# The gated unit of a state space branch: output blocks in the outer loop, chunks of positions inside

## The chip, the cores and the metric

The kernel runs on one core of a Trainium2 chip. The metric is device time in microseconds (us). The engines are TensorE (PE, with its weight loads as PEld), VectorE (DVE), ScalarE (ACT), GpSimd (POOL) and SyncE (SP). Each engine takes its instructions in the order in which they were written into its own queue; SP's queue issues most of the DMAs, ACT's and POOL's queues issue some.

## The reference, cut to what matters

One inference step of a one-layer decoder trunk, for a prompt of 1024 positions and 8 sample positions, 1032 in all. One branch of the layer is a diagonal state space scan followed by a gated unit; only the unit's last lines are touched here:

```
y = y.reshape(nb, seq_len, SSM_WIDTH) + d_skip.astype(f32) * uf
y = jax.nn.gelu(y)
y = y * jax.nn.sigmoid(y @ w_glu.astype(f32) + b_glu.astype(f32))
```

SSM_WIDTH is 512, so `w_glu` is 512 x 512. The branch's output is later multiplied by `w_ssm_proj`, gated and merged with an attention branch.

## The kernel before, in words

Positions are handled in three chunks of 344 (`NCH` = 3, `CH` = 344). A product in full precision is made of three products of rounded parts: every float32 operand is split into a high part (a cast on ACT, line 143 for weights) and a low part (a subtraction on DVE, line 144), and `mm3` issues high x high, high x low and low x high for each slice of 128 inputs (line 158). A block of weights comes through `loadw`: a DMA from SP (line 139) into one of two raw buffers, `r0` and `r1` in turn, then the cast and the subtraction into one of four pairs of buffers (`w2`/`w3`, `w4`/`w5`, `w6`/`w7`, `w8`/`w9`, in turn). A raw buffer is free for the next load when its subtraction is done; a pair is free when the matmuls of the block that used it are done. While pieces of a large cache copy are left, `loadw` also puts one of them into ACT's queue (line 868) with each load.

The program runs in stages: a first feed-forward part, the state space scan in eight batches (which writes `y` to `y_d` in DRAM), then `head(0, 0)` (query, key and value tiles of the first attention head pair), then `glu`, then six attention units, each with the `head` of the next one between its steps, then `ssm_proj` and the rest. `glu` loops over the three chunks. For each it loads the chunk of `y` (`yc`, 128 x 4 x 344, 688 KB), splits it into `yh` and `yl` in four pieces each (lines 547 and 548), and then, for each of four output blocks, loads the 512 x 128 block of `w_glu` (256 KB), multiplies (12 matmuls into one of three `pm` banks), takes tanh on ACT (line 553), multiplies by `y` on DVE (line 554) and stores the 128 x 344 result to `yg_d` from SP (line 555). The result tile `sg` has two buffers. So each block of `w_glu` is loaded and split three times, twelve loads in all. `ssm_proj` reads `yg_d` back much later (line 1165, tiles `P`).

The order of the instructions on each engine is not only that of the code: a scheduler merges `glu` with the tail of `head(0, 0)`, with the first steps of the first attention unit (`unit`, lines 645 to 690) and with the weight loads of `head(0, 1)` (`in_w_in`, 512 KB each), and fixes the order when the program is built.

Of the kernel before, what the change touches and what calls it, by code (L numbers as in the profile page):

```python
# [8 lines left out]
F32 = mybir.dt.float32  # L9
F32R = mybir.dt.float32r  # L10
I32 = mybir.dt.int32
AF = mybir.ActivationFunctionType
ALU = mybir.AluOpType
# [5 lines left out]
CH = 344  # L19
NCH = 3  # L20
# [39 lines left out]
class Step:  # L60
# [88 lines left out]

    def mm3(s, p, W, A, kts, first=True, last=True):  # L150

        nc = s.nc
        h, l = W
        n = 3 * len(kts)
        i = 0
        for kw, ka in kts:
            for w, a in ((h, A[0]), (h, A[1]), (l, A[0])):
                nc.tensor.matmul(p, w[:, kw], a[:, ka], start=first and i == 0, stop=last and i == n - 1)  # L158
                i += 1

    def dense(s, W, c, kts=None, A=None):
        p = s.pm.tile([128, 512], F32, name="pm")
        s.mm3(p[:, :CH], W, A or (s.ah[c], s.al[c]), kts or [(k, k) for k in range(KT)])
        return p[:, :CH]
# [6 lines left out]
    def ffn(s, hp, tmp, wg, wu, wd, xT, after, fill=None, lg=4):  # L171
# [17 lines left out]
        def down(fs):  # L189
            W = [s.loadw(wd[0][128 * f:128 * f + 128, :].rearrange("p (m q) -> p m q", q=128)) for f in fs]  # L190
            last = fs[-1] == NF - 1
            if last:
                order = [(m, c) for c in range(NCH) for m in range(KT)]
            else:
                order = [(m, c) for m in range(KT) for c in range(NCH)]
            for m, c in order:
                p = s.pm.tile([128, 512], F32, name="pm")[:, :CH]
                for i, f in enumerate(fs):
                    s.mm3(p, W[i], H[f], [(m, c)], i == 0, i == len(fs) - 1)
                nc.vector.scalar_tensor_tensor(xT[c][:, m], p, 0.5, xT[c][:, m], op0=ALU.mult, op1=ALU.add)  # L200
                if last:
                    after(c, m)
# [335 lines left out]
    def glu(s, gp):  # L538

        nc = s.nc  # L540
        for ch in range(NCH):
            cs = slice(CH * ch, CH * ch + CH)
            y = gp.tile([128, 4, CH], F32, name="yc", bufs=2)
            nc.sync.dma_start(y, s.y_d.rearrange("(m p) n -> p m n", p=128)[:, :, cs])
            yh, yl = gp.tile([128, 4, CH], F32R, name="yh", bufs=2), gp.tile([128, 4, CH], F32R, name="yl", bufs=2)
            for m in range(4):
                nc.scalar.copy(yh[:, m], y[:, m])
                nc.vector.tensor_sub(yl[:, m], y[:, m], yh[:, m])
            for m in range(4):
                W = s.colw(s.i['w_glu'], 128 * m, 4)  # L550
                p = s.dense(W, ch, [(k, k) for k in range(4)], (yh, yl))
                t = gp.tile([128, CH], F32, name="sg", bufs=2)
                nc.scalar.activation(t, p, AF.Tanh, bias=s.bglu[:, m:m + 1], scale=0.5)
                nc.vector.scalar_tensor_tensor(t, t, 1.0, y[:, m], op0=ALU.add, op1=ALU.mult)
                nc.sync.dma_start(s.yg_d[128 * m:128 * m + 128, cs], t)

    def ssm_finish(s, sp):
        nc = s.nc
# [1146 lines left out]
```

## Time and profile before

| | |
|---|---|
| median of three runs | 2382.05 us (2378.92 to 2386.34) |
| profiled execution, its own time | 2376.9 us |
| its span | 2375.0 us |
| PE busy / PEld busy | 97% / 93% of the span |
| DVE / ACT / POOL busy | 57% / 33% / 14% |
| mean granted clock of TensorE | 0.986 of full speed |

The table is read as follows. PE is the engine that is nearly always busy, and the other engines matter where PE waits for them. The share of 97% is an average over stages. A matmul's end is modelled in the records, and neighbours overlap, so a stretch with PE "busy" throughout can still hold more or fewer matmuls; counting them is the surer way. The profiled execution is 5.15 us below the median of the three runs.

### The profile page before, as it was taken

What the parts mean: (1) busy time and instruction counts of PE and PEld (TensorE: products, weight loads), DVE (VectorE), ACT (ScalarE), POOL (GpSimd) and SP (SyncE); (2) the same over time, 40 slices, a digit from 0 to 9 for tenths busy, and PEclk for the clock granted to TensorE, in tenths of its full rate; (3) what the DMA queues carried; (4) which work ended last, traced back from release to release, by engine and by line L of the source; (5) the groups of instructions that cost most, each with busy time, mean ns of one, the idle gap of its engine ahead of it and who ended that gap; (6) DMA issues with size and microseconds to landing.
All of it is one profiled execution on the core that took longest, in us unless ns stands there. A gap on an engine that the chain in (4) does not pass through costs nothing.

```text
span 2375.0 us, 37141 instructions
## 1 busy us (share of the span) xinstructions
PE 2296.6 (97%) x14409; PEld 2203.8 (93%) x14409; DVE 1359.9 (57%) x2929; ACT 787.7 (33%) x1506; POOL 337.0 (14%) x929
## 2 busy tenths in 40 slices
PE   7999999999999889989999998999999999999999
PEld 6999999999999889978888887899899999999999
DVE  7655544354433734455566536488866666664564
ACT  6211112111112434455443533235433333333222
POOL 3056777000000300000000000210000000000100
PEclk8999999999999999999999999999999999999999
DMA  5333334242323367561142126667334334367553
GB/s 141 101 102 115 110 113 132 85 122 82 112 77 121 129 171 223 176 214 33 57 119 76 40 87 174 219 233 233 116 125 129 119 119 149 119 256 265 193 174 126
DMA packets 300198, 325.73 MB, mean 137 GB/s; under 512 B 38822, under 2 KB 265494, under 8 KB 297462
## 3 DMA queue, kind: packets, MB, share of 16 engines
q1 hardware_dynamic: 277478, 189.94, 26.8%
q0 software_dynamic: 18864, 85.21, 10.1%
q10 hardware_dynamic: 3680, 48.22, 6.6%
q8 instruction: 113, 1.85, 0.3%
q14 instruction: 63, 0.52, 0.1%
HBM read 243.52 MB, written 123.78 MB: 155 GB/s over the span
## 4 chain that ended last, share of the span: by engine, by line
PE 65%; issue 21%; DMA 5%; DVE 5%; POOL 2%; ACT 1%; SPq 0%; ACTq 0%; POOLq 0%; DVEq 0%
PE pm L158 49%; PE pm L1560 9%; PE ps L671 2%; POOL hs_d L1376 2%; DMA r<-in_w_o_dram 1%; PE acc L687 1%; PE pT L680 1%; DMA r<-in_w_in_dram 1%; PE pn L972 1%; DVE xn L128 1%; DMA P<-yg_d 1%; DVE w L144 1%; DMA r<-in_w_ssm_proj_dram 1%; DMA w<-w_d 0%; DMA xr<-in_x_prompt_dram 0%
## 5 line engine op out<-in xcount | busy, mean ns | idle before, releaser
L158 PE MATMUL pm<-ah,w 128*128 128x344 f32 x4192 | 1006.8, 324 | 19.4 <-ACT ut L1141 11.0
L158 PEld LDWEIGHTS pm<-ah,w 128*128 128x128 f32 x4192 | 725.4, 189 | 37.6 <-ACT ut L1141 11.3
L158 PE MATMUL pm<-al,w 128*128 128x344 f32 x2384 | 719.3, 324 | 5.8 <-ACT al L1173 3.1
L158 PEld LDWEIGHTS pm<-al,w 128*128 128x128 f32 x2384 | 441.9, 190 | 13.1 <-issue 6.8
L158 PE MATMUL pm<-hh,w 128*128 128x344 f32 x1056 | 253.7, 321 | 0.0
L143 ACT CAST w<-r 128x1024 fp32r<-128x1024 f32 (+1 forms) x124 | 120.5, 978 | 373.8 <-PE pm L158 350.9
L144 DVE TENSOR_TENSOR w<-r,w 128x1024 fp32r<-128x1024 f32 (+1 forms) x124 | 142.6, 1152 | 159.3 <-ACT w L143 153.8
L1242 ACT CAST w<-r 128x1024 fp32r<-128x1024 f32 (+1 forms) x130 | 125.7, 968 | 286.8 <-PE pm L1348 171.4
L158 PEld LDWEIGHTS pm<-hh,w 128*128 128x128 f32 x1056 | 183.6, 188 | 0.4
L1348 PE MATMUL pm<-ah,w 128*128 128x344 f32 x1056 | 181.8, 320 | 1.2 <-ACT ah L1242 0.7
L1348 PE MATMUL pm<-e,w 128*128 128x344 f32 x1056 | 178.7, 320 | 1.0 <-DVE w L1243 1.0
L200 DVE SCALAR_TENSOR_TENSOR xT<-pm,xT 128x344 f32<-128x344 f32 x240 | 122.0, 515 | 93.4 <-PE pm L158 93.2
L1243 DVE TENSOR_TENSOR w<-r,w 128x1024 fp32r<-128x1024 f32 (+1 forms) x130 | 145.6, 1121 | 48.9 <-ACT w L1242 48.6
L1348 PEld LDWEIGHTS pm<-ah,w 128*128 128x128 f32 x1056 | 169.3, 188 | 1.8 <-ACT ah L1242 1.0
L1348 PEld LDWEIGHTS pm<-e,w 128*128 128x128 f32 x1056 | 168.6, 188 | 1.5 <-DVE w L1243 1.3
L158 PE MATMUL pm<-hl,w 128*128 128x344 f32 x528 | 169.5, 321 | 0.0
L184 DVE TENSOR_TENSOR h<-h,pm 128x344 f32<-128x344 f32 x66 | 33.8, 512 | 189.1 <-PE pm L158 189.1
L1348 PE MATMUL pm<-al,w 128*128 128x344 f32 x792 | 137.6, 322 | 2.6 <-ACT p L1428 2.6
L1348 PEld LDWEIGHTS pm<-al,w 128*128 128x128 f32 x792 | 128.0, 189 | 3.4 <-ACT p L1428 2.9
L158 PEld LDWEIGHTS pm<-hl,w 128*128 128x128 f32 x528 | 99.1, 188 | 0.2
L1376 POOL DMA_DIRECT2D hs_d<-hs x55 | 37.6, 683 | 426.4 <-DVE hs L1243 412.4
L1180 POOL DMA_DIRECT2D rs<-g_d x24 | 12.9, 541 | 532.6 <-DVE rs L103 389.5
(426 smaller groups left out, 3022.9 us busy)
## 6 DMA issues: line engine op xcount, KB each, us to landing
out_dram<-in_cache_kv_w_dram ACTq DMA_DIRECT2D x64, 512.0 KB
hs_d<-hs POOLq DMA_DIRECT2D x44, 688.0 KB, 4.5
r<-in_w_gate_dram SPq DMA_DIRECT2D x44, 512.0 KB
r<-in_w_up_dram SPq DMA_DIRECT2D x44, 512.0 KB
r<-in_w_in_dram SPq DMA_DIRECT2D x38, 512.0 KB
r<-in_w_down_dram SPq DMA_DIRECT2D x36, 512.0 KB
r<-in_w_o_dram SPq DMA_DIRECT2D x24, 512.0 KB
al<-hs_d POOLq DMA_DIRECT2D x7, 1376.0 KB, 6.7
```

What stands on the lines that cost most here:

```text
L128: nc.vector.scalar_tensor_tensor(xn, xT[c][:, k], s.gains[:, z, k:k + 1], r, op0=ALU.mult, op1=ALU.mult)
L143: nc.scalar.copy(h[:, :k], raw[:, :k])
L144: nc.vector.tensor_sub(l[:, :k], raw[:, :k], h[:, :k])
L158: nc.tensor.matmul(p, w[:, kw], a[:, ka], start=first and i == 0, stop=last and i == n - 1)
L184: nc.vector.tensor_mul(h, h, pu)
L200: nc.vector.scalar_tensor_tensor(xT[c][:, m], p, 0.5, xT[c][:, m], op0=ALU.mult, op1=ALU.add)
L671: nc.tensor.matmul(p[h][:, :nk], qT[hs, s.block(g, b)], kT[hs, ks], start=True, stop=True)
L1242: s.nc.scalar.copy(hi, x)
L1243: s.nc.vector.tensor_sub(lo, x, hi)
L1348: nc.tensor.matmul(p, W[w][:, k], B[:, a, k], start=first and k == 0 and z == 0, stop=k == n - 1 and z == 2, skip_group_check=True)
L1376: nc.gpsimd.dma_start(s.hs_d[i:i + n, j].rearrange("i p z n -> p i (z n)"), t[:, :n].rearrange("p i z n -> p i (z n)").bitcast(F32))
L1560: nc.tensor.matmul(p[m], W[wz][:, m], t[:, jj, az], start=e == 0 and k == 0, stop=e == n - 1 and k == 2, skip_group_check=True)
```

## The change

The loop over the four output blocks goes outside and the loop over the three chunks inside. All three chunks of `y` are loaded and split first, each with one cast and one subtraction over 128 x 1376 (through `parts`, lines 1242 and 1243 of the kernel before), and stay on chip, and each block of `w_glu` is loaded once and used for all three chunks. The result tile `sg` has four buffers and not two.

```diff
     def glu(s, gp):
 
         nc = s.nc
+        Y, P = [], []
         for ch in range(NCH):
-            cs = slice(CH * ch, CH * ch + CH)
-            y = gp.tile([128, 4, CH], F32, name="yc", bufs=2)
-            nc.sync.dma_start(y, s.y_d.rearrange("(m p) n -> p m n", p=128)[:, :, cs])
-            yh, yl = gp.tile([128, 4, CH], F32R, name="yh", bufs=2), gp.tile([128, 4, CH], F32R, name="yl", bufs=2)
-            for m in range(4):
-                nc.scalar.copy(yh[:, m], y[:, m])
-                nc.vector.tensor_sub(yl[:, m], y[:, m], yh[:, m])
-            for m in range(4):
-                W = s.colw(s.i['w_glu'], 128 * m, 4)
-                p = s.dense(W, ch, [(k, k) for k in range(4)], (yh, yl))
-                t = gp.tile([128, CH], F32, name="sg", bufs=2)
+            y = gp.tile([128, 4, CH], F32, name=f"yc{ch}")
+            nc.sync.dma_start(y, s.y_d.rearrange("(m p) n -> p m n", p=128)[:, :, CH * ch:CH * ch + CH])
+            yh, yl = (gp.tile([128, 4, CH], F32R, name=f"{x}{ch}") for x in ("yh", "yl"))
+            s.parts(y, yh, yl)
+            Y.append(y)
+            P.append((yh, yl))
+        for m in range(4):
+            W = s.colw(s.i['w_glu'], 128 * m, 4)
+            for ch in range(NCH):
+                p = s.dense(W, ch, [(k, k) for k in range(4)], P[ch])
+                t = gp.tile([128, CH], F32, name="sg", bufs=4)
                 nc.scalar.activation(t, p, AF.Tanh, bias=s.bglu[:, m:m + 1], scale=0.5)
-                nc.vector.scalar_tensor_tensor(t, t, 1.0, y[:, m], op0=ALU.add, op1=ALU.mult)
-                nc.sync.dma_start(s.yg_d[128 * m:128 * m + 128, cs], t)
+                nc.vector.scalar_tensor_tensor(t, t, 1.0, Y[ch][:, m], op0=ALU.add, op1=ALU.mult)
+                nc.sync.dma_start(s.yg_d[128 * m:128 * m + 128, CH * ch:CH * ch + CH], t)
```

The changed file has one line more, so lines behind the loop carry a number higher by one. What the scheduler makes of it is seen at three places.

The first place is SP's queue from the load of the fourth weight block on. `yc` are loads of `y`, `r0` and `r1` the raw buffers of weights, `yg_d` the stores of the unit. Before:

```order
L139 DMA r1_10767<-in_w_glu_dram 128x4x128
L544 DMA yc_10683<-y_d_59 128x4x344
L544 DMA yc_10791<-y_d_59 128x4x344
L139 DMA r0_10803<-in_w_glu_dram 128x4x128
L139 DMA r1_10827<-in_w_glu_dram 128x4x128
L139 DMA r0_10851<-in_w_glu_dram 128x4x128
L555 DMA yg_d_60<-sg_10715 128x344
L139 DMA r1_10875<-in_w_glu_dram 128x4x128
L555 DMA yg_d_60<-sg_10739 128x344
L139 DMA r0_10911<-in_w_glu_dram 128x4x128
L555 DMA yg_d_60<-sg_10763 128x344
L139 DMA r1_10935<-in_w_glu_dram 128x4x128
```

And of the change:

```order
L139 DMA r1_10875<-in_w_glu_dram 128x4x128
L544 DMA yc0_10683<-y_d_59 128x4x344
L544 DMA yc1_10689<-y_d_59 128x4x344
L544 DMA yc2_10695<-y_d_59 128x4x344
L139 DMA r0_11158<-in_w_in_dram 128x8x128
L139 DMA r1_11298<-in_w_in_dram 128x8x128
L556 DMA yg_d_60<-sg_10721 128x344
L556 DMA yg_d_60<-sg_10738 128x344
L139 DMA r0_11438<-in_w_in_dram 128x8x128
L556 DMA yg_d_60<-sg_10755 128x344
```

The third chunk of `y` moves up behind the second, eight loads of `w_glu` are gone, and the weights of `head(0, 1)` (`in_w_in`) take their places in the queue.

The second place is ACT's queue at the first results of the unit: `sg` is the tanh that empties a `pm` bank, CAST the high part of a weight block. Before:

```order
L143 CAST w2_10806<-r0_10803 128x512
L553 ACTIVATE sg_10715<-pm_10702,bglu_103 128x344
L868 DMA out_8_dram<-in_cache_kv_w512_dram 16x8160
L970 ACTIVATE rs0_10507<-kT_10436 128x344
L143 CAST w4_10830<-r1_10827 128x512
L553 ACTIVATE sg_10739<-pm_10726,bglu_103 128x344
L868 DMA out_8_dram<-in_cache_kv_w512_dram 16x8192
L143 CAST w6_10854<-r0_10851 128x512
L99 ACTIVATE rs0_10511<-pT_10509,eps_90 128x344
L100 ACTIVATE rs1_10512<-rs0_10511,seed_92 128x344
L553 ACTIVATE sg_10763<-pm_10750,bglu_103 128x344
```

And of the change:

```order
L554 ACTIVATE sg_10721<-pm_10708,bglu_103 128x344
L971 ACTIVATE rs0_10507<-kT_10436 128x344
L554 ACTIVATE sg_10738<-pm_10725,bglu_103 128x344
L143 CAST w2_11161<-r0_11158 128x1024
L554 ACTIVATE sg_10755<-pm_10742,bglu_103 128x344
L869 DMA out_8_dram<-in_cache_kv_w512_dram 16x8160
L99 ACTIVATE rs0_10511<-pT_10509,eps_90 128x344
L100 ACTIVATE rs1_10512<-rs0_10511,seed_92 128x344
L554 ACTIVATE sg_10779<-pm_10766,bglu_103 128x344
L101 ACTIVATE rs2_10513<-rs1_10512 128x344
L554 ACTIVATE sg_10796<-pm_10783,bglu_103 128x344
```

Before, a cast of a `w_glu` block stands ahead of every tanh. After, one cast of a twice as large `w_in` block stands ahead of every third tanh, the one of the last chunk.

The third place is SP's queue in `ssm_proj`, some 450 us later, where `P` are the loads of `yg_d`, `w_d` and `w` belong to the attention's `combine`, and `g_d` are stores of gates. Before:

```order
L1165 DMA P_15292<-yg_d_60 128x4x86
L959 DMA g_d_61<-gt_15096 128x344
L1165 DMA P_15302<-yg_d_60 128x4x86
L1165 DMA P_15304<-yg_d_60 128x4x86
L736 DMA w_d_63<-cw_15024 16x384
L959 DMA g_d_61<-gt_15124 128x344
L1165 DMA P_15314<-yg_d_60 128x4x86
L750 DMA w_15037<-w_d_63 64x4x128 x2
```

And of the change:

```order
L1166 DMA P_15226<-yg_d_60 128x4x86
L1166 DMA P_15236<-yg_d_60 128x4x86
L960 DMA g_d_61<-gt_15030 128x344
L1166 DMA P_15238<-yg_d_60 128x4x86
L737 DMA w_d_63<-cw_14958 16x384
L1166 DMA P_15248<-yg_d_60 128x4x86
L960 DMA g_d_61<-gt_15058 128x344
L751 DMA w_14971<-w_d_63 64x4x128 x2
```

Two loads of `P` move ahead of a store of gates. Elsewhere behind the unit, too, instructions of the same kinds change places by a few positions; none is added or removed there but the pieces of the cache copy, which follow the loads.

## Rows read from the trace of the kernel before

**Rows 1.** The page: span, and busy time of PE

```profile
span 2375.0 us, 37141 instructions
PE 2296.6 (97%) x14409; PEld 2203.8 (93%) x14409; DVE 1359.9 (57%) x2929; ACT 787.7 (33%) x1506; POOL 337.0 (14%) x929
```

**Rows 2.** Busy time of each engine by stretch of 40 us

```profile
core 0: us, PE busy (x) PEld busy (x) DVE busy (x) ACT busy (x) POOL busy (x), PEclk, DMA share, GB/s
...
980.00:1020.00 40.00, 40.00 (x254) 39.18 (x253) 22.61 (x49) 21.68 (x46) 0.19 (x1) 1.00 0.47 139
1020.00:1060.00 40.00, 29.67 (x170) 25.81 (x169) 24.22 (x53) 18.73 (x35) 0.00 (x0) 1.00 0.84 260
1060.00:1100.00 40.00, 40.00 (x259) 32.79 (x258) 24.45 (x75) 23.97 (x66) 0.00 (x0) 1.00 0.16 47
```

**Rows 3.** What PE waited for, 1015 to 1061 us

```profile
PE pm L158 <- ACT sg L553: 5.1, 5, 2.0
PE pT L647 <- DVE sk L645: 3.2, 1, 3.2
```

**Rows 4.** Timeline of ACT: start us, length us, instruction, idle before it

```profile
1002.69 0.48 ACT L547 CAST yh<-yc 128x344 fp32r<-128x344 f32 x1 [2.14 <-DMA yc<-y_d]
...
1004.61 1.61 ACT L547 CAST yh<-yc 128x344 fp32r<-128x344 f32 x4
...
1025.67 0.62 ACT L143 CAST w<-r 128x512 fp32r<-128x512 f32 x1 [5.15 <-PE pm L158]
...
1027.26 0.53 ACT L553 ACTIVATE sg<-pm,bglu 128x344 f32<-128x344 f32 x1
...
1046.05 1.04 ACT L143 CAST w<-r 128x1024 fp32r<-128x1024 f32 x1 [2.15 <-DMA r<-in_w_in_dram]
```

**Rows 5.** Timeline of SP's queue: issues of DMAs

```profile
998.41 1.00 SPq L544 DMA_DIRECT2D yc<-y_d  x2
...
1020.91 0.37 SPq L139 DMA_DIRECT2D r<-in_w_glu_dram  x1
...
1029.43 1.24 SPq L139 DMA_DIRECT2D r<-in_w_glu_dram  x1
...
1041.19 0.38 SPq L139 DMA_DIRECT2D r<-in_w_in_dram  x1
```

**Rows 6.** Timeline of PE

```profile
1015.38 0.58 PE L158 MATMUL pm<-yh,w 128*128 128x344 f32 x1
...
1027.84 0.42 PE L158 MATMUL pm<-yh,w 128*128 128x344 f32 x1 [2.03 <-ACT sg L553]
...
1033.99 1.04 PE L612 MATMUL pT<-ident,vT 128*128 128x128 f32 x8
...
1050.29 0.43 PE L158 MATMUL pm<-ah,w 128*128 128x344 f32 x1 [0.53 <-ACT sg L553]
...
1059.49 0.28 PE L647 MATMUL pT<-ident,sk 128*24 128x128 f32 x1 [3.19 <-DVE sk L645]
1059.70 0.90 PE L671 MATMUL ps<-kT,qT 64*128 64x256 f32 x4
1060.53 0.43 PE L158 MATMUL pm<-ah,w 128*128 128x344 f32 x1
```

**Rows 7.** The chain that ended last, 960 to 1110 us: start us, us, what

```profile
1015.81 6.44 PE pm L158 x41
1022.25 0.58 PE pT L972 x2
```

**Rows 8.** What PE waited for, 1061 to 1460 us

```profile
PE acc L687 <- ACT P L682: 1.3, 1, 1.3
```

**Rows 9.** Instructions of line 1242: count, ns min/median/max, first and last start

```profile
L1242 ACT CAST al<-xT x3: 1332/1347/1350, 1622.6 to 1649.2; 128x1376 fp32r<-128x1376 f32 x3
```

**Rows 10.** Busy time by stretch, as rows 2, in `ssm_proj`

```profile
1460.00:1500.00 40.00, 31.43 (x181) 25.34 (x180) 25.30 (x58) 14.03 (x34) 2.15 (x4) 0.85 0.51 122
```

**Rows 11.** The chain that ended last, 1440 to 1520 us

```profile
1491.84 4.51 DMA P<-yg_d
```

## The prediction

> **What bounds the kernel now.** I read the page first: PE is busy for 2296.6 of 2375.0 us [rows 1], so a change pays only where PE stands still. The table of stretches says where that is around the gated unit: in 1020 to 1060 us PE is busy for 29.67 of 40 us, with full stretches on either side and the granted clock at 1.00 in all three [rows 2]. So 10.33 us are idle by the record, and no clock is lost there.
>
> What PE waits for there is the tanh on ACT that empties its banks, 5.1 us in five waits, and at the end the small copies `sk` on DVE, 3.2 us in one [rows 3]. Both are late because of weights. On ACT's timeline a cast of a `w_glu` block starts at 1025.67 after 5.15 us of idling; the view names PE as the releaser, but the cast's data came from a load that SP had issued only about 6 us before, so I put this wait down to the load. The tanh that PE needed stands behind that cast and starts at 1027.26 [rows 4], and PE goes on at 1027.84 after 2.03 us [rows 6]. SP's timeline shows the period: raw buffer `r1` is loaded at 1020.91 and again, two loads later in the queue, at 1029.43 [rows 5]. One buffer turns round in 8.5 us (load, cast, subtraction, wait), two buffers give a block every 4.3 us. A block is used by only 12 matmuls. From the chain, 41 matmuls take 6.44 us [rows 7], 0.157 us each, so 12 take 1.9 us. PE uses up weights more than twice as fast as they come. That is the bound of this stage: the turnaround of two raw buffers.
>
> **What the change does to it, part by part.** First, what the stage costs beyond its matmuls, by counting.
>
> The unit's first matmul starts at 1015.38, the first one of the next head (`ah`, behind the unit in PE's order) at 1050.29 [rows 6]: 34.91 us. In between lie 144 matmuls of the unit (12 blocks of 12), 144 x 0.157 = 22.6 us; two products with `bones` at 0.58, 1.2 us [rows 7]; eight transposes, 1.04 us; one pair of score products, at most the 0.90 us that a later pair takes [rows 6]. Sum 25.7 us, lost 9.2 us.
>
> From 1050.29 to 1060.53, 10.24 us, the order holds 33 matmuls of the head (5.2 us), the transpose of `sk` (0.28 us) and a pair of score products (0.90 us): 6.4 us, lost 3.9 us. The two losses make 13.1 us. The record's 10.3 us is less because a matmul behind a wait counts as busy for 0.42 us though its successors start every 0.157. I take the count.
>
> *Eight of twelve weight loads, casts and subtractions go.* The four blocks that stay are the four that were already in place or on their way when the unit began (their loads stand ahead of `yc` in both orders), and each now feeds 36 matmuls, 5.7 us. So PE does not wait for `w_glu` at all. ACT saves 8 x 0.62 = 5.0 us [rows 4], and DVE the subtractions; neither is a gain of its own, both engines have idle time in this stage [rows 2].
>
> *The weights of the next head move up.* Their loads now stand directly behind `yc2`. A load takes 1046.05 - 1041.19 = 4.9 us from issue to cast [rows 4, 5], in a stage where the DMA engines are busy for 0.84 of the time [rows 2]; the change takes 8 x 256 KB of weights and the cache pieces that went with them out of it. The first can be issued when the third `w_glu` block is split, well before 1015, and its cast needs the first pair of weight buffers, free after 36 matmuls at about 1021. The second waits for the fourth `w_glu` block, whose pair is free when the value tile's matmuls end at about 1015: issue near 1017, landed near 1022, cast when block two is done, near 1027. From there each has 5.7 us of matmuls for a load of 4.9 us that starts after the cast and the subtraction of the one two before. I count no wait.
>
> *The third chunk of `y` moves up.* Two chunks are issued from 998.41 on [rows 5]; the first is used at 1002.69, the second by 1004.61 [rows 4]. One more of 688 KB costs at most the 4.3 us of the first, so it lands by 1008.9. Its cast over 128 x 1376 takes 1.35 us [rows 9], three of them 4.0 us against 12 x 0.48 = 5.7 us before. PE wants it at 1015.38 + 24 x 0.157 = 1019.2. The cover is the tail of `head(0, 0)`, some 9 us; behind this cast on ACT stand the copies that empty the banks of the value tile, wanted by PE from 1015 on, so a late chunk would first show there.
>
> *Stores get four buffers.* A store may now take as long as four results, 7.5 us. This is part of the 13.1 us already.
>
> *The cache pieces* that went with the removed loads go with later ones, where the DMA share is 0.16 [rows 2]. I cost them at nothing; that idle DMA time is the cover.
>
> So the gain is 13.1 us at most. For waits that stay I take a bound of 0 on one side and on the other the longest wait that PE meets in the following 400 us, 1.3 us [rows 8]; between them 0.7 us, since the walk above found none but rests on durations that another order may stretch. Behind the unit PE is the bound up to 1460 and the gain is carried on. **Sum: 13.1 - 0.7 = 12.4 us.** The profiled execution took 2376.9 us, so 2364.5; it lies 5.15 us below the median of the runs, so the forecast for the median is 2369.7 us, 0.5% less than before.
>
> **A rule that speaks against it.** Above each third tanh of the unit there is now a cast twice as long, and this cast cannot start before PE has finished the block. The row shows what that does: the tanh at 1027.26 waited for the cast in front of it [rows 4]. [...] What it would do here is the first rival.
>
> **Rivals.**
>
> *ACT's order holds the banks.* After a block's last matmul the cast takes 1.04 us and the tanh behind it 0.53 us [rows 4], 1.6 us in all. PE can fill two other banks meanwhile, 24 x 0.157 = 3.8 us, so each cast may be 2.2 us late. If the loads of `w_in` come as late as the worst one of before, 5.15 us, three casts cost 3 x (5.15 - 2.2) = 8.9 us: gain 3.5, median 2378.5. Against it speaks the walk above, in which they land with some 5 us to spare. Chance 0.08.
>
> *The wait for `sk` stays.* The copies still stand on DVE behind the subtraction of the fourth `w_in` block. Then only the first loss goes: 9.2 us, 2372.9. For it: it is the longest single wait of before. Against it: in the new order 47 matmuls of the head, 7.4 us, lie between the unit's end and the transpose of `sk`, before 33, and the fourth load can be issued some 10 us before the unit ends. Chance 0.14.
>
> *The stage of `ssm_proj` shifts.* PE is idle there for 8.57 us and the clock falls to 0.85 [rows 10], because the loads of `P` go one after another through SP's queue, up to 4.51 us each [rows 11]. The order of just these loads changes by some places. It can give up to 8.6 us more (then 2361 to 2367, chance 0.12), since two loads stand earlier, or take some of the gain, say 6 us (2375.7, chance 0.12).
>
> *The same stage turns the sign.* To end measurably slower it has to lose 12.4 + 7.1 = 19.5 us, that is more than four further loads of 4.51 us each laid bare. Sixteen loads pass through two buffers, so five is possible: 22.6 us more than the forecast, a median of 2392.3. From the fifth load on it decides. Against it: in the new order the loads stand earlier, not later. Chance 0.04.
>
> **How the numbers follow.** Measurements of this kernel tell about 0.3%, 7.1 us, from no change, so "faster" is below 2374.9. The forecast itself has 0.50; its own range is 2369.0 (no wait left) to 2371.6 (two waits of 1.3 us). Faster are this, the wait for `sk` (0.14), the better `ssm_proj` (0.12) and a small part of the worse one (0.03): 0.79. The same are the rest of that (0.09) and the rival on ACT (0.08): 0.17. Slower: 0.04. The range takes in `sk` and most of both `ssm_proj` cases: 2362 to 2377.
>
> **What the profile after will show.** If right: PE busy for nearly all of the 40 us from 1015 on, the first matmul of `head(0, 1)` near 1041 and not 1050; no wait of PE for a tanh of more than 0.5 us; four loads of `w_glu` and the first `w_in` load before 1015; casts of `w_in` that wait for PE, not for a DMA; and every later stage some 12 us earlier. It is wrong if PE waits for the tanh behind a `w_in` cast, if the copies of the value tile on ACT wait for `yc2`, or if the lead of 12 us at 1100 is gone at 1500.

## The result, and the profile after

| | before | after |
|---|---|---|
| median of the timed runs | 2381.73 us (2378.92 to 2386.34, 6 runs) | 2363.86 us (2362.41 to 2368.49, 6 runs) |
| profiled execution, its own time | 2376.9 us | 2366.11 us |

The ratio is 0.9928 with a 95% interval of 0.9917 to 0.9939: faster by 17.9 us in the medians, 14.5 to 19.8 by the interval. The forecast was 2369.7 us, in a range of 2362 to 2377.

The busy time by stretch of the changed kernel, the view of [rows 2]:

```profile
core 0: us, PE busy (x) PEld busy (x) DVE busy (x) ACT busy (x) POOL busy (x), PEclk, DMA share, GB/s
980.00:1020.00 40.00, 40.00 (x255) 39.18 (x254) 23.21 (x43) 21.86 (x40) 0.19 (x1) 1.00 0.49 149
1020.00:1060.00 40.00, 40.00 (x252) 37.87 (x251) 26.23 (x60) 21.97 (x45) 0.00 (x0) 1.00 0.58 176
1060.00:1100.00 40.00, 40.00 (x270) 33.11 (x268) 23.88 (x72) 22.65 (x57) 0.00 (x0) 1.00 0.13 38
```

The middle stretch is full: 252 matmuls where before had 170, and the DMA engines fall from 0.84 to 0.58. Between 1005 and 1070 us the view of PE's waits has no row at all, where before had 8.3 us in six waits for the tanh and for `sk` [rows 3] and 2.1 us in four others.

PE's timeline, as in [rows 6]: the first matmul of the unit, the last one, the first of the next head, and the transpose of `sk`.

```profile
1017.88 0.58 PE L158 MATMUL pm<-yh,w 128*128 128x344 f32 x1
...
1043.35 0.32 PE L158 MATMUL pm<-yh,w 128*128 128x344 f32 x1
1043.50 0.32 PE L158 MATMUL pm<-ah,w 128*128 128x344 f32 x1
...
1050.89 0.27 PE L648 MATMUL pT<-ident,sk 128*24 128x128 f32 x1
```

From 1017.88 to 1043.50 it is 25.62 us, where the prediction counted 25.7 us of work. From there to `sk` it is 7.39 us, where it counted 47 matmuls in 7.4. The unit itself starts 2.5 us later than before, in an execution that holds 159 matmuls from 820 to 860 us where the one of before holds 175 (16 x 0.157 = 2.5 us); a second profile of before holds 160 there, so this is not the change.

ACT's timeline, as in [rows 4], the casts of `y` and of the weights; the two over 128 x 512 are of `w_glu`, the four over 128 x 1024 of `w_in`:

```profile
1005.13 1.34 ACT L1243 CAST yh<-yc 128x1376 fp32r<-128x1376 f32 x1 [2.07 <-DMA yc<-y_d]
...
1006.97 1.34 ACT L1243 CAST yh<-yc 128x1376 fp32r<-128x1376 f32 x1
...
1008.22 0.61 ACT L143 CAST w<-r 128x512 fp32r<-128x512 f32 x1
...
1009.07 1.35 ACT L1243 CAST yh<-yc 128x1376 fp32r<-128x1376 f32 x1
...
1017.60 0.62 ACT L143 CAST w<-r 128x512 fp32r<-128x512 f32 x1 [0.47 <-PE pm L158]
...
1023.84 1.05 ACT L143 CAST w<-r 128x1024 fp32r<-128x1024 f32 x1 [1.18 <-PE pm L158]
...
1030.10 1.05 ACT L143 CAST w<-r 128x1024 fp32r<-128x1024 f32 x1 [0.81 <-PE pm L158]
...
1037.23 1.05 ACT L143 CAST w<-r 128x1024 fp32r<-128x1024 f32 x1 [1.18 <-PE pm L158]
...
1043.55 1.05 ACT L143 CAST w<-r 128x1024 fp32r<-128x1024 f32 x1 [1.82 <-PE pm L158]
```

The third chunk is cast from 1009.07 to 1010.42 without a wait for its load, some 11 us ahead of its use (1017.88 + 24 x 0.157 = 1021.6). The casts of `w_in` wait for PE to release a pair of buffers and not for a load. SP's queue issues the two first loads of `w_in` from 1010.90 on:

```profile
1000.76 1.55 SPq L544 DMA_DIRECT2D yc<-y_d  x3
1010.90 8.73 SPq L139 DMA_DIRECT2D r<-in_w_in_dram  x2
```

**A measure for the stage.** The order of matmuls behind the unit differs between kernels, so one instruction that stands in all of them serves as the far end: the transpose of `sk` in the fifth attention unit. In the profile before and in that after it is

```profile
1347.18 0.27 PE L647 MATMUL pT<-ident,sk 128*24 128x128 f32 x1
```

```profile
1336.08 0.27 PE L648 MATMUL pT<-ident,sk 128*24 128x128 f32 x1
```

From the unit's first matmul that is 1347.18 - 1015.38 = 331.8 us before [rows 6], and 1336.08 - 1017.88 = 318.2 after. This length, called the stage below, is free of what an execution lost earlier or loses later, and holds the same 1969 matmuls in every kernel below.

### The profile page after: what moved, and what is told of

Same layout as the page of the kernel before. It is cut to its first block, busy times and chain, and to the rows that moved or that the text cites. A ratio compares the mean times of both kernels' runs of the same rounds, so it can differ in the third digit from the quotient of the medians.

```text
span 2364.3 us, 37070 instructions
## 1 busy us (share of the span) xinstructions
PE 2293.4 (97%) x14409; PEld 2203.6 (93%) x14409; DVE 1355.7 (57%) x2912; ACT 782.6 (33%) x1489; POOL 336.0 (14%) x929
## 4 chain that ended last, share of the span: by engine, by line
PE 65%; issue 22%; DMA 5%; DVE 4%; POOL 2%; ACT 1%; SPq 1%; POOLq 0%; ACTq 0%; DVEq 0%
PE pm L158 49%; PE pm L1561 9%; PE ps L672 2%; POOL hs_d L1377 2%; DMA rs<-g_d 1%; PE acc L688 1%; PE pT L681 1%; DMA r<-in_w_o_dram 1%; PE pn L973 1%; DVE xn L128 1%; DMA xr<-in_x_prompt_dram 1%; DMA w<-w_d 0%; DMA P<-yg_d 0%; PE pT L811 0%; PE pT L457 0%
## 5 line engine op out<-in xcount | busy, mean ns | idle before, releaser
L143 ACT CAST w<-r 128x1024 fp32r<-128x1024 f32 (+1 forms) x116 | 115.6, 1004 | 357.2 <-PE pm L158 341.8
L144 DVE TENSOR_TENSOR w<-r,w 128x1024 fp32r<-128x1024 f32 (+1 forms) x116 | 137.1, 1184 | 146.5 <-ACT w L143 145.9
L1243 ACT CAST w<-r 128x1024 fp32r<-128x1024 f32 (+1 forms) x130 | 125.6, 968 | 282.6 <-PE pm L1349 172.2
L1244 DVE TENSOR_TENSOR w<-r,w 128x1024 fp32r<-128x1024 f32 (+1 forms) x130 | 145.5, 1121 | 50.7 <-ACT w L1243 50.1
L185 ACT CAST hh<-h 128x344 fp32r<-128x344 f32 x66 | 31.5, 478 | 169.6 <-DVE h L184 169.6
```

The costliest lines, as they stand in the source:

```text
L143: nc.scalar.copy(h[:, :k], raw[:, :k])
L144: nc.vector.tensor_sub(l[:, :k], raw[:, :k], h[:, :k])
L185: nc.scalar.copy(hh[:, c], h)
L1243: s.nc.scalar.copy(hi, x)
L1244: s.nc.vector.tensor_sub(lo, x, hi)
```

## Experiments

Theory: the twelve loads of `w_glu` through two raw buffers set the pace. Rivals: the DMA engines, 0.84 busy in 1020 to 1060 us [rows 2] (contention with the cache pieces), the two result buffers with their stores, or the order of the loops. Twelve runs were made, in three groups of four; each group shares its runs of the kernel before. All results first, with the one above as "after" ("unit" is from its first matmul to the first of the next head; every length comes from that kernel's one profile):

| kernel | unit us | stage us | median us | ratio to before, 95% interval |
|---|---|---|---|---|
| before | 34.91 | 331.8 | 2381.73 | |
| before, second profile | 37.95 | 333.4 | | |
| before, third profile | 35.68 | 334.3 | | |
| four raw buffers | 35.74 | 332.9 | 2377.47 | 0.9982 (0.9973 to 0.9992) |
| after's loops, twelve loads | 32.84 | 331.4 | 2373.66 | 0.9964 (0.9950 to 0.9977) |
| no cache pieces | 31.41 | 327.4 | 2375.41 | 0.9969 (0.9956 to 0.9982) |
| four result buffers | 34.24 | 327.1 | 2372.68 | 0.9965 (0.9952 to 0.9978) |
| more buffers of three kinds | 25.31 | 322.5 | 2370.46 | 0.9946 (0.9930 to 0.9962) |
| after, two result buffers | 27.65 | 320.2 | 2369.16 | 0.9947 (0.9931 to 0.9963) |
| four loads kept, chunks outside | 26.17 | 319.8 | 2366.70 | 0.9932 (0.9920 to 0.9944) |
| the same, four result buffers | 26.17 | 318.5 | 2365.84 | 0.9933 (0.9919 to 0.9947) |
| after, `P` from POOL's queue | 25.63 | 318.8 | 2364.83 | 0.9928 (0.9915 to 0.9942) |
| after | 25.62 | 318.2 | 2363.86 | 0.9928 (0.9917 to 0.9939) |
| after, again | 25.66 | 317.8 | 2362.73 | 0.9915 (0.9902 to 0.9928) |

**The changed kernel again.** No edit.

> The changed kernel once more, unaltered, beside the others of this group. If the gain of 17.9 us between the medians is real, 2362 to 2366 us; if the part above the 13 us that the stage accounts for was chance, 2367 to 2370.

It took 2362.73 us against 2380.64 for before in its group: 17.9 us again. The stage is 317.8 us.

**Four raw buffers** for the loads of `w_glu`, otherwise before:

```diff
-        raw = s.wsl(f"r{n % 2}", dt=F32)
+        raw = gp.tile([128, 4, 128], F32, name=f"gr{n % 4}") if gp else s.wsl(f"r{n % 2}", dt=F32)
...
-                W = s.colw(s.i['w_glu'], 128 * m, 4)
+                W = s.loadw(s.i['w_glu'][0].rearrange("(k p) f -> p k f", p=128)[:, :, 128 * m:128 * m + 128], 4, gp=gp)
```

> Before, with four raw buffers of its own for the loads of w_glu and all twelve loads left. Turnaround theory: 8.5 us over four buffers is a block every 2.1 us against 1.9 us of matmuls, so most of the first loss goes, and r0 and r1 are free for w_in: gain 6 to 11, 2371 to 2376 us. Rival, the DMA engines (busy 0.84 of the stretch) are the limit and not the two buffers: gain below 3, 2379 to 2383.

2377.47 us, and a stage of 332.9 us, which is that of before. The theory's gain of 6 to 11 us isn't there, and the 3.2 us of the medians lie just above the rival's bound of 3. (Its granted clock is 0.91 in 1020 to 1060 us and 0.92 in the next 40; the third profile of before, with 0.90 and 0.93 there, has a stage of 334.3 us.) The waits of PE and, in a second view, two tanh and the third chunk on ACT's timeline tell why:

```profile
PE pm L158 <- ACT sg L553: 4.4, 3, 2.2
PE pT L647 <- DVE sk L645: 3.1, 1, 3.1
PE pm L158 <- ACT yh L547: 1.9, 1, 1.9
```

```profile
1028.41 0.55 ACT L553 ACTIVATE sg<-pm,bglu 128x344 f32<-128x344 f32 x1 [3.43 <-DMA yg_d<-sg]
...
1039.70 0.48 ACT L547 CAST yh<-yc 128x344 fp32r<-128x344 f32 x1 [2.26 <-DMA yc<-y_d]
...
1048.53 0.55 ACT L553 ACTIVATE sg<-pm,bglu 128x344 f32<-128x344 f32 x1 [2.58 <-DMA yg_d<-sg]
```

PE still waits for a tanh, but the tanh no longer waits behind a cast without data: it waits for the store of the result two before it. The wait for a weight became a wait for a result buffer, then one for the third chunk, then `sk` as before. So two raw buffers were not the only bound, and not one that decides alone.

**More buffers of three kinds**: four raw buffers as above, and

```diff
-            y = gp.tile([128, 4, CH], F32, name="yc", bufs=2)
+            y = gp.tile([128, 4, CH], F32, name="yc", bufs=3)
...
-                t = gp.tile([128, CH], F32, name="sg", bufs=2)
+                t = gp.tile([128, CH], F32, name="sg", bufs=4)
```

> Before with twelve loads of w_glu, but four raw buffers for them, four result buffers and three buffers for the chunk of y: all the waits for a buffer that the run with four raw buffers showed are taken away at once. Chain of buffers (each wait taken away laid the next one bare): the unit runs near PE's pace, gain 7 to 12, 2369 to 2374 us. Rival, the DMA engines are too full for twelve loads with the cache pieces: the loads stay late, gain below 4, 2377 to 2382.

2370.46 us, as the chain of buffers has it. With all twelve loads the unit takes 25.31 us, PE's own pace. So the DMA engines, with a share of 0.79 in 1020 to 1060 us, do not hold the unit by themselves. What is left is behind it: `sk` waits while the weights of the next head are loaded as late as before (the first two issued at 1040.93 and 1045.16, before at 1041.19 and 1042.92).

```profile
PE pT L647 <- DVE sk L645: 2.3, 1, 2.3
```

**Four result buffers** alone, in the kernel before:

```diff
-                t = gp.tile([128, CH], F32, name="sg", bufs=2)
+                t = gp.tile([128, CH], F32, name="sg", bufs=4)
```

> Before with four result buffers, nothing else. Turnaround theory: two waits of the tanh for a store, 2.3 us on ACT, go, but the weights still set the pace: within 3 us of before, 2378 to 2384. Rival, the stores hold the banks: gain above 5, below 2376.

2372.68 us, 8.6 us less than before in its group where the theory had at most 3: this rival's number. The stage is 6.1 us shorter than the mean of the three profiles of before (333.2). Both buffers matter, and the result buffers hide what more raw buffers are worth: more raw buffers alone give 0.3 us of the stage, more result buffers alone a part.

**No cache pieces** with the loads of `w_glu`, the only ones that hand `gp` to `loadw`; the pieces go with later loads:

```diff
-        s.shift()
+        if not gp:
+            s.shift()
```

> Before, but the twelve loads of w_glu issue no piece of the cache copy (the pieces go with later loads). Two raw buffers as limit with a load's own latency: a load comes down from 4.9 us to perhaps 3.5, the turnaround from 8.5 to 7, a block every 3.5 us: gain 3 to 6, 2375 to 2378 us. Rival, contention with the cache pieces is the cause of the losses: gain 9 to 13, 2368 to 2372. If the pieces cost nothing: 2379 to 2383.

2375.41 us, at the lower end of the theory's 2375 to 2378. The DMA share of the stretch falls from 0.84 to 0.67:

```profile
1020.00:1060.00 40.00, 32.89 (x186) 29.42 (x186) 24.75 (x57) 21.67 (x45) 0.00 (x0) 0.96 0.67 203
```

The first load of `w_in` takes 4.3 us from issue to cast there (1035.33 to 1039.60), where it took 4.9. The loads of `w_glu` gain more. In the kernel before, SP's issues of a load that its cast waits for and of the last block, and that cast:

```profile
1027.04 0.37 SPq L139 DMA_DIRECT2D r<-in_w_glu_dram  x1
...
1035.87 0.37 SPq L139 DMA_DIRECT2D r<-in_w_glu_dram  x1
```

```profile
1032.24 0.62 ACT L143 CAST w<-r 128x512 fp32r<-128x512 f32 x1 [3.11 <-DMA r<-in_w_glu_dram]
```

And without the pieces, SP's issues of the block ahead of it, of the same load and of the last block, and the cast:

```profile
1019.90 0.37 SPq L139 DMA_DIRECT2D r<-in_w_glu_dram  x1
...
1022.49 0.37 SPq L139 DMA_DIRECT2D r<-in_w_glu_dram  x1
...
1029.32 0.37 SPq L139 DMA_DIRECT2D r<-in_w_glu_dram  x1
```

```profile
1025.38 0.62 ACT L144 CAST w<-r 128x512 fp32r<-128x512 f32 x1 [0.54 <-DMA r<-in_w_glu_dram]
```

From issue to cast it is 2.9 us, where before took 5.2, and the last five blocks are issued every 2.4 us (1019.90 to 1029.32, four periods), where before took 3.7 (1020.91 [rows 5] to 1035.87). So with the cache pieces each turn of the ring is longer, and taking them away is worth 5.8 us of the stage (327.4 us against the mean of 333.2). It is not the whole: with weights at that pace PE still waits 3.8 us for two tanh and 2.5 us for `sk`.

**The changed loops with twelve loads**:

```diff
-            W = s.colw(s.i['w_glu'], 128 * m, 4)
             for ch in range(NCH):
+                W = s.colw(s.i['w_glu'], 128 * m, 4)
```

> The changed kernel with the load moved into the inner loop: blocks outside, all parts of y on chip, four result buffers, but twelve loads of w_glu again. Turnaround theory: the stage runs at 4.3 us per block again and everything is lost: 2378 to 2385 us. Rival, order of loops, parts on chip and result buffers bring a part themselves: 2364 to 2375.

2373.66 us: about 7 us better than before, the rival's range. SP's timeline shows two raw buffers taking a block every 3.2 us on average (1022.03 to 1034.74, four periods), not the 4.3 that the prediction took from the turn in [rows 5]:

```profile
1022.03 0.37 SPq L139 DMA_DIRECT2D r<-in_w_glu_dram  x1
...
1025.23 0.39 SPq L139 DMA_DIRECT2D r<-in_w_glu_dram  x1
...
1028.48 0.38 SPq L139 DMA_DIRECT2D r<-in_w_glu_dram  x1
...
1032.80 0.38 SPq L139 DMA_DIRECT2D r<-in_w_glu_dram  x1
...
1034.74 0.38 SPq L139 DMA_DIRECT2D r<-in_w_glu_dram  x1
```

With four blocks there before the start, that pace nearly feeds the unit: its matmuls end at 1043.94, 27.56 us behind the first. The price of the loads then falls on the next head, whose first matmul waits for its weight:

```profile
1043.94 0.32 PE L158 MATMUL pm<-yh,w 128*128 128x344 f32 x1
...
1049.22 0.65 PE L158 MATMUL pm<-ah,w 128*128 128x344 f32 x1 [4.97 <-ACT w L143]
```

Its one profile took 2378.84 us, the highest of its six runs, and its granted clock of 1240 to 1300 us, inside the stage, is 0.91. So its stage of 331.4 us is no fair match for its median.

**Four loads kept, chunks outside**:

```diff
+        Ws = [s.colw(s.i['w_glu'], 128 * m, 4) for m in range(4)]
         for ch in range(NCH):
...
-                W = s.colw(s.i['w_glu'], 128 * m, 4)
-                p = s.dense(W, ch, [(k, k) for k in range(4)], (yh, yl))
+                p = s.dense(Ws[m], ch, [(k, k) for k in range(4)], (yh, yl))
```

> Chunks outside as before, but the four blocks of w_glu are loaded and split once and stay in their four pairs of buffers. Turnaround theory: eight loads are gone, so both losses (9.2 and 3.9 us) go as in the changed kernel, less 1 to 2 us because the third chunk of y is still loaded late: 2368 to 2372 us. Rival, the order of the loops (or y on chip) is what counts: within 4 us of before, 2378 to 2385.

2366.70 us, a little better than the theory's 2368 to 2372 and far from the rival. Without the eight loads, with two result buffers and the third chunk late, 13.4 of the 15.2 us of the stage are there. PE's only wait is 0.8 us for `sk`. This is the main part of the change.

**The same with four result buffers**:

```diff
-                t = gp.tile([128, CH], F32, name="sg", bufs=2)
+                t = gp.tile([128, CH], F32, name="sg", bufs=4)
```

> The chunks outside, four loads of w_glu kept, and four result buffers. If fewer loads and more result buffers are the whole cause and the order of the two loops is none of it: as the changed kernel, 2362 to 2366 us. If blocks outside (which lets the weights of the next head come earlier) is a part of it: 2366 to 2370, as with two result buffers.

2365.84 us, stage 318.5 us. Its interval (0.9919 to 0.9947) overlaps with that of both runs of the changed kernel. So chunks outside or inside makes no difference that these runs can tell.

**The changed kernel with two result buffers**:

```diff
-                t = gp.tile([128, CH], F32, name="sg", bufs=4)
+                t = gp.tile([128, CH], F32, name="sg", bufs=2)
```

> The changed kernel with two result buffers. A result comes every 1.9 us, so a tanh, product and store may take 3.8 us. Theory (weights alone): no change, 2361 to 2365 us. Rival, the chain of buffers: in a stage without waits for weights the tanh waits for the store of two results before, up to 3.4 us as with four raw buffers, and PE for the tanh: 2366 to 2374.

2369.16 us, the rival's range: 5 to 6 us of the medians go. In the stage it is 2.2 us, no more than the 2.5 by which the three profiles of before differ. On ACT the tanh waits for stores in six places, where the changed kernel has two of 1.7 us in all; PE, with two further banks to fill, sees only 1.7 us of it in three waits:

```profile
ACT sg L554 <- DMA yg_d<-sg: 11.2, 6, 2.8
```

**`P` from POOL's queue**, in the changed kernel:

```diff
-                    nc.sync.dma_start(y, s.yg_d[128 * m:128 * m + 128, 512 * hf:512 * hf + 512].rearrange(
+                    nc.gpsimd.dma_start(y, s.yg_d[128 * m:128 * m + 128, 512 * hf:512 * hf + 512].rearrange(
```

> The changed kernel with the loads of P (the read of the unit's result in ssm_proj) issued from the queue of GpSimd and not of SyncE, where they stand behind stores and the loads of combine. If their place in that queue is what PE waits for late (4.6 and 5.6 us for al in two executions): gain 3 to 8 on the changed kernel, 2355 to 2361. If the two buffers of P are, or the queue of GpSimd holds them up instead: 2361 to 2372.

2364.83 us: no gain. Of PE's wait for `al` in `ssm_proj`, 4.6 us in the changed kernel's profile, 3.7 us are still there, so its place in SP's queue is not what holds `P` most, unless POOL's queue held it as long. On POOL's timeline a load of `P` waits 4.76 us for DVE, which reads the two buffers of `P`, the longest of these waits between 1450 and 1500 us:

```profile
1486.53 0.75 POOL L1166 DMA_DIRECT2D P<-yg_d  x1 [4.76 <-DVE al L1175]
```

That points at the two buffers; a run with more of them was not made. No version beat the changed kernel.

**Before, a second and a third profile**:

> The kernel before, unaltered, for a second profile. The profile of before that the prediction worked from took 2376.9 us, below every timed run of it at that point. If that execution was untypically quick in the gated unit itself, another one of some 2381 us loses 3 to 5 us more between the unit's first matmul and 1310 us; if it was quick elsewhere, the stage costs the same and the difference lies in other stretches.

> The same for a third profile, with the same two expectations.

They took 2380.74 and 2377.02 us, with stages of 333.4 and 334.3 us, 1.6 and 2.5 more than the first, where 3 to 5 or nothing was expected. The second execution is the longer one mainly because it reaches the unit 4.2 us later (1019.53 against 1015.38), so neither expectation holds. In both the granted clock of 1020 to 1060 us is below full, 0.91 and 0.90, where [rows 2] shows 1.00:

```profile
1020.00:1060.00 40.00, 31.09 (x174) 28.65 (x173) 23.51 (x47) 20.88 (x40) 0.00 (x0) 0.91 0.79 242
```

```profile
1020.00:1060.00 40.00, 31.81 (x169) 28.59 (x167) 23.96 (x52) 18.56 (x34) 0.00 (x0) 0.90 0.84 258
```

PE's timeline of the third profile shows one such place, and the second view its clock:

```profile
1027.51 0.42 PE L158 MATMUL pm<-yh,w 128*128 128x344 f32 x1 [1.89 <-ACT sg L553]
...
1027.95 0.78 PE L158 MATMUL pm<-yh,w 128*128 128x344 f32 x2
...
1031.36 0.48 PE L158 MATMUL pm<-yh,w 128*128 128x344 f32 x2
```

```profile
1024.00:1027.00 3.00, 1.62 (x11) 1.34 (x9) 0.69 (x1) 1.63 (x4) 0.00 (x0) 1.00 0.64 212
1028.00:1031.00 3.00, 3.00 (x12) 3.00 (x11) 1.74 (x5) 0.79 (x2) 0.00 (x0) 0.50 0.64 210
1032.00:1034.00 2.00, 2.00 (x12) 1.51 (x12) 1.32 (x3) 1.82 (x4) 0.00 (x0) 1.00 0.89 242
```

Behind the wait for the tanh the clock is at 0.50, and 3 us hold 12 matmuls. In the first profile the same 3 us hold 20, at 1.00, after a wait of 2.03 us [rows 6]:

```profile
1028.00:1031.00 3.00, 3.00 (x20) 3.00 (x21) 2.08 (x5) 1.13 (x3) 0.00 (x0) 1.00 0.92 258
```

## Why the prediction was right, and where not

**The loss in the stage.** Counted: 9.2 and 3.9 us, 13.1 in all. Measured against the same profile: 331.8 - 318.2 = 13.6 us, and 14.0 for the second profile of the change. The count of matmuls was right to within 0.5 and 0.9 us, and it did not depend on what caused the loss.

**Waits that stay.** 0.7 us were taken off; PE has no wait there. With this the forecast of 12.4 us was 1.2 to 1.6 us short in the stage.

**What the profile cannot show alone.** The prediction said that no clock is lost there, which holds for one execution of three. Over three, the stage of before takes 333.2 us, over two that of the change 318.0: a gain of 15.2. That the clock fell behind a wait of PE in one profile (0.50 in 1028 to 1031 us of the third), and that it stays at 1.00 in 1020 to 1060 us in both of the change, was left out of the sum. The mean stage is 1.4 us longer than the one counted; that the clock makes this difference is argued, since the waits differ between the executions too.

**The bound.** The step that failed is "That is the bound of this stage: the turnaround of two raw buffers". It was the longest turn read as the period (the last five blocks of the same profile come every 3.7 us and not 4.3), and one ring of several: raw buffer, result buffer with its store, chunk of `y`, and the same two raw buffers for the next head, on two queues and on DMA engines that are 0.84 full [rows 2]. In both queues the work of the lists starts in their order in the profile before: SP's twelve DMAs from 996.70 to 1029.43 us, ACT's nine casts and activations from 1017.58 to 1027.26. Against the mean of before, four raw buffers give 0.3 us of the stage, no cache pieces 5.8, result buffers alone 6.1, three kinds together 10.7, and fewer loads alone 13.4. The loads are the common cause, since they take raw buffers, places in SP's and ACT's queues and DMA time at once. The forecast of a gain was right because the change removes the loads, whichever of their effects binds.

**The parts.** Eight loads less: shown, the largest part. The weights of the next head move up: their casts wait for PE only (0.81 to 1.82 us), as forecast, and with twelve loads they are what PE waits for, 4.97 us. The first was issued at 1010.90, ahead of 1015 as forecast, the second by 1019.63 where the forecast had 1017. The third chunk of `y`: hidden, as forecast. Four result buffers: said to be part of the 13.1; undone, they cost 2.2 us of the stage, which is within the scatter of profiles, and 5 to 6 us of the medians, which is not. The first matmul of the next head comes 25.6 us behind the unit's first, as counted; "near 1041" became 1043.50 since this execution reached the unit late.

**Rivals.** ACT's order does not hold the banks: the four tanh behind a cast of `w_in` start 0.95 us after it (1024.79 behind 1023.84, the last 1044.50 behind 1043.55), and PE waits for none of them. The wait for `sk` is gone, and so is the loss of 3.9 us. The stage of `ssm_proj`: from the fifth `sk` to the last product of `oh` with the attention's weights the three profiles of before take 234.2 to 236.9 us, the two of the change 238.3 and 240.1. Some 4 us go there, and PE's waits in the first profile of the change have `al`, the input made from `P`, with 4.6 us as the longest:

```profile
PE pm L158 <- ACT al L1174: 4.6, 1, 4.6
```

From there to the end the change takes 788.1 and 787.5 us, before 790.9 to 791.4: a stretch at a lower clock near 2140 us, 0.91 over 40 us in the first profile of before, is at 1.00 in both of the change. The two nearly cancel. Two other kernels with the change's gain (four loads kept with four result buffers, and `P` from POOL's queue) take 234.6 and 233.9 us in the first part and 793.0 and 791.9 in the second, so I read both as scatter of order and clock and not as effects of the change. But five kernels with a part of the gain take 237.2 to 239.5 us in the first part, so that is not settled. The prediction would have been wrong if the lead of the changed kernel were gone at 1500 us. It is not: at the fifth `sk` the two profiles of the change are 11.1 and 13.2 us ahead of the first of before, at the end of the first part 7.8 and 11.7.

**What stays open.** The profiled executions differ by 14.3 us (mean spans 2376.4 and 2362.1), the medians by 17.9. The three profiled executions of before took 2376.9, 2380.74 and 2377.02 us against medians of 2380.6 to 2381.7 for its timed runs; those of the change lie on both sides of theirs. 3.6 us of the gain have thus no place in a trace. The interval (14.5 to 19.8) nearly reaches the profiled difference, so this may be chance in which executions were profiled. That the median of 2363.86 us lies in the forecast's range of 2362 to 2377 is in part luck: the sum by itself allowed 2369.0 to 2371.6, and the range reached below 2367 only for a better stage of `ssm_proj`, which did not come. The sum was 5.5 us short of the gain: 1.2 to 1.6 in the profiles that it was counted in, some 1.4 in how the stage scatters, and the rest without a cause shown.

## What to carry to other kernels

Where PE starves, count the work between two instructions and take the difference as the loss: that number held in the stage (13.1 us counted, 13.6 and 14.0 measured), while the story of the cause, drawn from the longest turn of one buffer, did not. When several small rings (raw tile, result tile, chunk) share queues and DMA engines, more buffers in one of them can just lay the next bare, as four raw buffers did here (0.3 us of the stage); taking the traffic away relieved all at once (13.4 us with eight loads fewer). Before such a count, take more than one profile of the kernel before: here the stage took 331.8, 333.4 and 334.3 us in three.

## What the runs showed of the hardware

The same program lost clock in some executions and not in others: of the three profiles of before, one keeps 1.00 through 1020 to 1060 us and two are at 0.91 and 0.90. PE's waits from 1005 to 1070 us differ, too: 5.1 us for the tanh and 3.2 us for `sk` in the first, 6.6 and 2.3 in the second, 4.7 and 2.9 in the third. A wait of 2.03 us was followed by a clock of 1.00 in the first, one of 1.89 us by 0.50 in the third, both in 1028 to 1031 us. Both profiles of the change, with no wait of PE there, stay at 1.00 in 1020 to 1060 us. The two executions that lost clock took 1.6 and 2.5 us more for the stage than the one that did not.

One load of 256 KB took 5.2 us from issue to cast with the DMA engines 0.84 busy in 1020 to 1060 us; the same load took 2.9 us with the cache pieces taken out and the share at 0.67.
